# A two-layer hybrid decoder on one core: the mask and the gates' sums by adding transfers, rotary tables from the start, and later places for tasks behind long chains

## The chip, the cores and the metric

One core of one Trainium2 chip runs the whole program. The metric is the device time of one execution in microseconds, the median of the timed runs. The core's engines are TensorE (PE, matmuls, with its weight loads shown apart as PEld), VectorE (DVE), ScalarE (ACT), GpSimd (POOL) and SyncE (SP, which only issues loads of weights); 16 DMA engines move data. Each engine executes its own instructions in the order in which the program lists them.

## The reference

Two layers, each a mixer of three head groups, a cross-attention to 256 memory tokens and a SwiGLU feed-forward, all with sandwich RMSNorm, for 256 tokens of width 1024:

```python
def forgetting_attention(q, k, v, f_logit, b_f):
    ...
    log_f = jax.nn.log_sigmoid((f_logit + b_f).astype(jnp.float32))
    c = jnp.cumsum(log_f, axis=1).transpose(0, 2, 1)
    ...
        logits = jnp.einsum('bhqd,bhkd->bhqk', qb, k).astype(jnp.float32) * scale + cb[..., None] - c[:, :, None, :]
        q_pos = start + jnp.arange(Q_BLOCK)
        mask = key_pos[None, :] <= q_pos[:, None]
        p = jax.nn.softmax(jnp.where(mask, logits, -jnp.inf), axis=-1)
        return jnp.einsum('bhqk,bhkd->bhqd', p.astype(v.dtype), v)

def rotary(x, positions):
    half = x.shape[-1] // 2
    inv_freq = ROPE_THETA ** (-jnp.arange(half, dtype=jnp.float32) / half)
    ang = positions.astype(jnp.float32)[..., None] * inv_freq
    cos = jnp.cos(ang)[:, :, None, :]
    sin = jnp.sin(ang)[:, :, None, :]
    ...

def parallel_mixer(h, positions, w_in, conv_w, conv_b, w_rg, b_rg, w_ig, b_ig, lru_lambda, fox_b_f, w_out):
    proj = h @ w_in
    lx, ly, fq, fk, fv, ff, rq, rk, rv, rg = jnp.split(proj, np.cumsum(SPLIT_SIZES)[:-1].tolist(), axis=-1)
    lru_out = rg_lru(causal_depthwise_conv(lx, conv_w, conv_b), w_rg, b_rg, w_ig, b_ig, lru_lambda) * jax.nn.gelu(ly)
    fox_out = forgetting_attention(fq, fk, fv, ff, fox_b_f)
    ret_out = retention(rq, rk, rv, rg, positions)
    return jnp.concatenate([lru_out, fox_out.astype(h.dtype), ret_out], axis=-1) @ w_out
```

`retention` rotates its queries and keys by `rotary` before it multiplies them. The forgetting attention has 8 heads in blocks of 128 queries; a query sees no key after itself.

## The kernel before

Weights stream from DRAM in pieces of 128 partitions by 1024 floats (512 KB), issued on SP's queue into five raw buffers. Every piece is split into two parts that the matmuls can take with little loss: ACT makes `hi` (a cast of `raw`), DVE makes `lo` (`raw` minus `hi`). A product is then three matmuls: activation times hi, activation times lo, and the activation's own lower part times hi. There are eight pairs of hi and lo buffers, so pieces can be split some time ahead of their use.

The order of all instructions is found by a planner while the program is built (`Flow`). It keeps a clock for each engine, with estimated costs, and a heap of tasks, which are generators. A task that yields tensors is woken once the planner's clock of TensorE has passed the time at which it expects them to be written; a task that yields a number is woken that much later (`MARGIN` is 3.0 us). In between, TensorE gets the matmuls of the projections. What a woken task issues stands at that place of each engine's list. On the chip the engines keep to the list and wait for what their operands need: a bad estimate shows as a wait of TensorE. `pump` splits the next weight piece where the planner sees ACT and DVE free.

The tasks that the change touches:

- `rotary_tables` (L603): the positions' cast `s` on DVE, angles and their reduction `ang` on POOL (some 25 small instructions), Sin twice on ACT (`cs`), copies to `c` on DVE, four transposes of `c` on TensorE, and `turn` from them. With it `use_rqk` (L1008) makes `rab`, `rcd` and `rot` on DVE for the retention's queries and keys, and the scores `rsc` on TensorE.
- `gates` (L826): after the softplus of the forget gates (`soft`, a chain of small DVE instructions), three matmuls `cum` make the sums over tokens, which go to DRAM (`dr`, `cum<-cT`) and come back on POOL's queue, broadcast to all partitions, as four `far` tiles of 256 KB.
- `fox` (L874): the forgetting attention's logits `lg`. For each half of the queries and two heads' banks, a matmul of the identity with the mask (`lg<-maskb`, bfloat16, 0 or -1e30) starts the sum, the query-key matmuls add to it, and DVE scales it and adds `far` (`pexp<-lg,f,far`), takes the maximum and, behind ACT's Exp, divides.
- `lru` (L946): four matmuls `gate` in two banks, one bank after the other.
- `flip` in `ffn` (L1197): transposes of the gated hidden rows `fg`; `spread` (L776): norms as rows, `rsb<-diag`.
- `memory_norm` (L1256): mean squares of a memory half (`junk`, `ss`, `rstd`), the scaling `msrc<-msrc,rstd` on ACT, then transposes `tr<-cst,msrc`.

Of the kernel before, what the change touches and what calls it, by code (L numbers as in the profile page):

```python
# [18 lines left out]
P = 128  # L19
# [12 lines left out]
WORK_BUFS = 25  # L32
# [6 lines left out]
LATE = 6  # L39
TAIL = 2  # L40
# [16 lines left out]
def _constants():  # L57

    i = np.arange(P)
    gamma = 1.0 - np.exp2(-5.0 - np.arange(4, dtype=np.float64))  # L60
    diff = np.arange(SEQ)[None, None, :] - i[:, None, None]
    dec = np.where(diff >= 0, gamma[None, :, None] ** np.maximum(diff, 0), 0.0) * HD ** -0.5
    dec = np.concatenate([dec, dec[:, :, 0:P]], axis=2)
    inv = np.broadcast_to(10000.0 ** (-np.arange(32, dtype=np.float64) / 32), (P, 32))
    m = np.where(i[None, :] <= i[:, None], 0.0, NEG)
    z = np.zeros_like(m)
    mask = np.concatenate([m, m, m, m, z, m, z, m, np.eye(P)], axis=1)
    f = [np.eye(P), i[:, None] <= i[None, :], np.ones((P, P)), dec.reshape(P, -1), inv]
    return [np.asarray(x, np.float32) for x in f], mask.astype(ml_dtypes.bfloat16)
# [56 lines left out]
class Flow:  # L126
# [39 lines left out]
    def load(self, queue, out, ins=()):  # L166
# [6 lines left out]
        if queue == "POOL":  # L173

            self.swdge = max(t, self.clock["POOL"], self.swdge) + 2.0 * cost
            self.write(out, self.swdge + 1.3)
# [44 lines left out]
class Engine:  # L221
# [5 lines left out]
    def __getattr__(self, op):  # L227
        fn = getattr(self.eng, op)

        def call(*args, **kw):  # L230
# [5 lines left out]
            if "dma" in op:  # L236
                fn(*args, **kw)
                self.flow.load(self.name, outs[0], aps)
                return
# [47 lines left out]
def decoder(ctx: ExitStack, tc: tile.TileContext, a, out):  # L287
# [173 lines left out]
    def pump(force=False, later=None):  # L461
# [12 lines left out]
        if force or (idle and not flow.hold) or (here and lead < (LEAD if not flow.hold else HOLD_LEAD)):  # L474
# [8 lines left out]
            split(hi[:, 0:m], lo[:, 0:m], b.parts[i], later)  # L483
# [83 lines left out]
    maskb = const([P, 1024 + P], BF16, n="maskb")  # L567
    identb = maskb[:, 1024:1024 + P]
# [34 lines left out]
    def rotary_tables():  # L603
        posf = small([P, NT])
        V.tensor_copy(posf, posi)
# [35 lines left out]
        cs = work([P, 2, NT, 32], n="cs")  # L641
        S.activation(cs[:, 1], s, AF.Sin, bias=0.0, scale=1.0)
# [4 lines left out]
        yield c4  # L647
        tb = transposes([c4[:, c, t].rearrange("p h j -> p (h j)") for c in range(2) for t in range(NT)])
# [127 lines left out]
    def spread(xt, got):  # L776
# [7 lines left out]
        yield d  # L784
        b = bank("rsb")
# [6 lines left out]
    def mixer(l, xt, blk, skew, between=None):  # L792
# [10 lines left out]
        def use_fv_hi(t, q):  # L803
# [16 lines left out]
            if l == 0:  # L820
                PO.tensor_scalar(sp4, lfs[:, 0:4], -4.0, None, op0=ALU.mult)
                PO.tensor_scalar(sp2, lfs[:, 0:4], -2.0, None, op0=ALU.mult)
# [3 lines left out]
        def gates():  # L826


            yield list(lf)
            b = bank("cum")  # L830
# [8 lines left out]
            yield dr  # L839
            for e in range(2):  # L840
                for g in range(2):
                    far[e, g] = work([P, 2, SEQ], n="far")
                    PO.dma_start(out=far[e, g], in_=dr[4 * e + 2 * g:4 * e + 2 * g + 2, :].partition_broadcast(P))
# [30 lines left out]
        def fox(u):  # L874
# [7 lines left out]
            for e in range(2):  # L882
                matmul(bs[e], identb, maskb[:, 512 * t:512 * t + 512], True, False)
            for i, j in enumerate(js):
                for e in range(2):
                    r = slice(64 * e, 64 * e + 64)
                    matmul(bs[e][:, i * w:(i + 1) * w], qT[j // 2][r, j % 2, t * P:(t + 1) * P],
                           kT[j // 2][r, j % 2, 0:w], False, i == n - 1)
            ps = []
            for e in range(2):  # L890
# [4 lines left out]
                for g in sorted(set(j // 2 for j in js)):  # L895
                    i = 2 * g - js[0]
                    V.scalar_tensor_tensor(pv[:, i:i + 2], bv[:, i:i + 2], xt[t].by[HD ** -0.5], far[e, g][:, :, 0:w],
                                           op0=ALU.mult, op1=ALU.add)
# [47 lines left out]
        def lru():  # L946
# [18 lines left out]
            for gate, dst in ((0, tr), (1, ti)):  # L965
                b = bank("gate")
                for c in range(2):
                    matmul(b[:, c * SEQ:(c + 1) * SEQ], bd[:, l, gate, c, :], xc[:, c, :], True, True)
                for c in range(2):
                    o = 4 * gate + 2 * l + c  # L970
                    S.activation(dst[:, c, :], b[:, c * SEQ:(c + 1) * SEQ], AF.Tanh, bias=hb[:, o:o + 1], scale=0.5)
                yield 0.6
# [206 lines left out]
    def ffn(xt, blk, make_post):  # L1179
# [17 lines left out]
        def flip(t, gg):  # L1197
            tb = transposes([gg[:, j * P:(j + 1) * P] for j in range(4)])
# [3 lines left out]
            return  # L1202
            yield
# [52 lines left out]
    def memory_norm(m):  # L1256
# [9 lines left out]
        yield MARGIN  # L1266
# [37 lines left out]
    def between(k):  # L1304
# [7 lines left out]
        if t:  # L1312
            PO.dma_start(out=maskb, in_=a["mask"])
# [52 lines left out]
```

## Time and profile before

| | |
|---|---|
| median of three timed runs | 832.49 us (831.71 to 832.66) |
| the profiled run | 832.4 us, of which the span of its instructions is 830.6 us |
| mean granted clock of TensorE | 0.998 |
| DMA | 147.50 MB, mean 178 GB/s; 260 to 305 GB/s in the first three of 40 slices |
| DVE, lo<-raw,hi | 246 instructions, 293.9 us, 1.2 us each |
| ACT, hi<-raw | 246 instructions, 251.9 us, 1.0 us each |
| POOL's own DMA queue | 2080 packets, 7.91 MB |

A row of the timeline gives the start and the duration of an instruction (of several that follow each other without another between them: the whole, with their count), its engine and its line, and in brackets how long the engine had been idle before and what it waited for. Nearly all lines are those of helpers (L242 for all calls on DVE, ACT and POOL, L320 for matmuls, L341 for transposes), so instructions are told apart by the names of their tiles. Matmuls are pipelined: what one costs is the distance between starts, not its own duration. "DMA to landing" is the time from a transfer's issue to its completion.

### The profile page before, as it was taken

How to read it: one execution, taken by the hardware profiler on the slowest of the kernel's cores; microseconds unless marked ns; L12 is line 12 of the kernel's file. 1: busy time of each engine (PE TensorE's matmuls, PEld its weight loads, DVE VectorE, ACT ScalarE, POOL GpSimd, SP SyncE). 2: the span in 40 equal slices, each digit the busy share in tenths (PEclk: the TensorE clock that was granted, in tenths of full speed). 3: DMA queues.
4: the chain of work that ended last, by engine and by line, in shares of the span. 5: the costliest groups of instructions: out<-in, count | busy, mean ns of one | idle time of the engine just before them, and what ended most of it. 6: DMA issues, size and time to landing. Idle time of an engine off the chain costs nothing.

```text
span 830.6 us, 12999 instructions
## 1 busy us (share of the span) xinstructions
PE 818.8 (99%) x5023; PEld 714.9 (86%) x5023; DVE 588.9 (71%) x854; ACT 450.6 (54%) x728; POOL 80.2 (10%) x136
## 2 busy tenths in 40 slices
PE   9989999999999999999999999999999999999996
PEld 6989977998888888888889998789988788888885
DVE  6578996867577766758678888566767775857663
ACT  5569465746366544645474376555545563554541
POOL 2752100200020000000041100010002000000000
PEclk9999999999999999999999999999999999999999
DMA  8883545563357846557447563446444765647411
GB/s 296 305 260 121 171 158 155 188 216 114 121 185 240 251 138 220 186 157 232 137 128 237 168 204 127 151 129 228 145 129 133 232 222 181 207 147 244 139 49 51
DMA packets 101885, 147.50 MB, mean 178 GB/s; under 512 B 4976, under 2 KB 79104, under 8 KB 101696
## 3 DMA queue, kind: packets, MB, share of 16 engines
q1 hardware_dynamic: 99040, 138.17, 52.1%
q0 software_dynamic: 2080, 7.91, 2.8%
q8 instruction: 39, 0.64, 0.3%
q10 hardware_dynamic: 704, 0.59, 0.2%
q14 instruction: 22, 0.18, 0.1%
HBM read 145.59 MB, written 1.06 MB: 177 GB/s over the span
## 4 chain that ended last, share of the span: by engine, by line
PE 89%; DMA 3%; POOL 2%; issue 2%; DVE 2%; ACT 1%; DVEq 0%; POOLq 0%; ACTq 0%
PE acc L320 55%; PE dn L320 25%; PE tr L341 3%; DMA raw<-in_w_in 2%; PE co L320 1%; PE clg L320 1%; DMA raw<-in_w_down 1%; PE lg L320 1%; ACT hi L242 1%; POOL ang L242 1%; PE fo L320 1%; DVE lo L242 1%; PE ry L320 1%; POOL f L242 0%; PE gate L320 0%
## 5 line engine op out<-in xcount | busy, mean ns | idle before, releaser
L242 DVE TENSOR_TENSOR lo<-raw,hi 128x1024 fp32r<-128x1024 f32 (+2 forms) x246 | 293.9, 1215 | 88.1 <-ACT hi L242 86.7
L320 PE MATMUL acc<-xt,hi 128*128 128x256 f32 (+1 forms) x1344 | 340.1, 332 | 0.0
L242 ACT CAST hi<-raw 128x1024 fp32r<-128x1024 f32 (+2 forms) x246 | 251.9, 1043 | 92.5 <-PE acc L320 59.8
L320 PE MATMUL acc<-xt,lo 128*128 128x256 f32 x960 | 259.1, 282 | 0.0
L320 PEld LDWEIGHTS acc<-xt,hi 128*128 128x128 f32 x1344 | 223.3, 189 | 20.9 <-issue 0.4
L320 PEld LDWEIGHTS acc<-xt,lo 128*128 128x128 f32 x960 | 181.2, 189 | 6.3
L320 PE MATMUL acc<-hi,xt 128*128 128x512 f32 (+2 forms) x320 | 83.6, 351 | 0.0
L320 PEld LDWEIGHTS acc<-hi,xt 128*128 128x128 f32 x320 | 56.1, 188 | 8.5 <-ACT hi L242 0.6
L242 POOL TENSOR_TENSOR rp<-ssp,mh 128x1 f32<-128x1 f32 x12 | 6.8, 567 | 573.1 <-DVE ssp L242 573.0
L320 PE MATMUL acc<-lo,xt 128*128 128x512 f32 (+2 forms) x160 | 54.1, 349 | 0.0
L320 PE MATMUL dn<-hi,mth 128*128 128x512 f32 x128 | 51.6, 403 | 0.0
L242 DVE TENSOR_TENSOR fs<-acc,fs 128x256 f32<-128x256 f32 x72 | 30.1, 418 | 29.0 <-ACT fs L242 29.0
L320 PE MATMUL dn<-hi,mtl 128*128 128x512 f32 x128 | 50.5, 394 | 0.0
L320 PE MATMUL dn<-lo,mth 128*128 128x512 f32 x128 | 50.5, 394 | 0.0
L320 PE MATMUL acc<-mem,hi 128*128 128x256 f32 x256 | 47.3, 285 | 0.0
L242 ACT COPY fs<-acc 128x256 f32<-128x256 f32 x72 | 26.2, 364 | 37.7 <-PE acc L320 37.7
L320 PE MATMUL acc<-hi,mem 128*128 128x512 f32 x128 | 45.1, 405 | 0.0
L320 PE MATMUL dn<-hi,gh 128*128 128x512 f32 x112 | 44.3, 396 | 0.0
L320 PE MATMUL dn<-hi,gl 128*128 128x512 f32 x112 | 44.2, 394 | 0.0
L320 PE MATMUL dn<-lo,gh 128*128 128x512 f32 x112 | 44.2, 394 | 0.0
L320 PEld LDWEIGHTS acc<-mem,hi 128*128 128x128 f32 x256 | 39.5, 189 | 1.4 <-issue 1.0
L242 DVE TENSOR_TENSOR y<-dn,gpost 128x512 f32<-128x512 f32 x24 | 16.4, 685 | 28.3 <-ACT junk L242 28.3
(206 smaller groups left out, 1168.7 us busy)
## 6 DMA issues: line engine op xcount, KB each, us to landing
raw<-in_w_gate SPq DMA_DIRECT2D x44, 512.0 KB, 4.8
raw<-in_w_up SPq DMA_DIRECT2D x44, 512.0 KB, 4.6
raw<-in_w_down SPq DMA_DIRECT2D x44, 512.0 KB, 4.7
raw<-in_w_in SPq DMA_DIRECT2D x42, 512.0 KB, 5.4
raw<-in_w_ck SPq DMA_DIRECT2D x16, 512.0 KB, 3.7
raw<-in_w_cv SPq DMA_DIRECT2D x16, 512.0 KB, 4.9
raw<-in_w_out SPq DMA_DIRECT2D x16, 512.0 KB, 4.1
raw<-in_w_cq SPq DMA_DIRECT2D x16, 512.0 KB, 4.5
```

The costliest lines, as they stand in the source:

```text
L242: fn(*args, **kw)
L320: nc.tensor.matmul(out_ap, lhsT, rhs, start=start, stop=stop)
L341: nc.tensor.transpose(out_ap, src, ident[0:k, 0:k])
```

## The change

Six things, all within the functions above:

1. The mask matmuls are gone, and with them the mask's load (288 KB) and its tiles. The mask is now a float array in DRAM. In `gates`, six `far` tiles of 256 KB (one per bank of `lg`) are loaded with mask rows first (1.5 MB a layer), and six transfers of the sums are added to them in the transfer itself (`accum_op=ALU.add`) in place of the four plain ones. DVE's `pexp<-lg,f,far` is one instruction of 512 columns where it was two of 256.
2. `pump` makes the lower part of a piece in another way where the planner sees DVE late (between 60 and 130 us of its clock, with three pieces ready): ACT writes `lo = -hi`, and a transfer from DRAM adds the weights to it. In the built program this holds for four pieces, one of w_in and three of w_out.
3. The cast of positions is done by POOL, so the rotary angles don't wait for their place on DVE; both Sin stand together, and a MARGIN is put ahead of the transposes of `c`.
4. More waiting in the planner: MARGIN ahead of the `cum` matmuls and of the gate matmuls (less 1.0; both banks' matmuls now together), 0.7 us ahead of `flip` and of the matmul of `rsb`, MARGIN + 2 in place of MARGIN in `memory_norm`.
5. Two small instructions move from POOL to DVE (`sp4`, `sp2`, printed as `spl`), and there are 26 work buffers in place of 25.
6. The planner's estimate of the landing of a transfer on POOL's queue is longer (3.0 in place of 1.3).

```diff
@@ -29,7 +28,7 @@
 SPLIT_BUFS = 8
-WORK_BUFS = 25
+WORK_BUFS = 26
 PIECE = 1056
@@ -37,6 +36,7 @@
 LATE = 6
+DVE_LATE, ADD_LEAD, ADD_FROM, ADD_TO = 4.0, 3, 60.0, 130.0
 TAIL = 2
@@ -64,9 +64,9 @@
     z = np.zeros_like(m)
-    mask = np.concatenate([m, m, m, m, z, m, z, m, np.eye(P)], axis=1)
+    mask = np.concatenate([m, m, m, m, z, m, z, m], axis=1)
     f = [np.eye(P), i[:, None] <= i[None, :], np.ones((P, P)), dec.reshape(P, -1), inv]
-    return [np.asarray(x, np.float32) for x in f], mask.astype(ml_dtypes.bfloat16)
+    return [np.asarray(x, np.float32) for x in f], mask.astype(np.float32)
@@ -173,7 +173,7 @@
             self.swdge = max(t, self.clock["POOL"], self.swdge) + 2.0 * cost
-            self.write(out, self.swdge + 1.3)
+            self.write(out, self.swdge + 3.0)
             self.clock["DMA"] += cost
@@ -235,7 +235,7 @@
                 fn(*args, **kw)
-                self.flow.load(self.name, outs[0], aps)
+                self.flow.load(self.name, outs[0], aps + outs * ("accum_op" in kw))
                 return
@@ -480,7 +480,15 @@
                 flow.free[hi.tensor.name] = flow.free[lo.tensor.name] = freed["split"].pop(0)
-            split(hi[:, 0:m], lo[:, 0:m], b.parts[i], later)
+            hm, lm = hi[:, 0:m], lo[:, 0:m]
+            if ADD_FROM < flow.now < ADD_TO and c["DVE"] > c["PE"] + DVE_LATE and lead >= ADD_LEAD and c["POOL"] < c["PE"] + 4.0:
+
+                S.copy(hm, b.parts[i])
+                S.activation(lm, hm, AF.Copy, bias=0.0, scale=-1.0)
+                r, c0 = b.cuts[i], b.at[i]
+                PO.dma_start(out=lm.rearrange("p (c n) -> p c n", c=r), in_=b.src[:, c0:c0 + r, :], accum_op=ALU.add)
+            else:
+                split(hm, lm, b.parts[i], later)
             freed["raw"].append(flow.ready(lo) or flow.ready(hi) + 2.0)
@@ -564,8 +572,6 @@
     bd = cst[:, C_BD:C_END].rearrange("p (l g c j) -> p l g c j", l=DEPTH, g=2, c=2)
-    maskb = const([P, 1024 + P], BF16, n="maskb")
-    identb = maskb[:, 1024:1024 + P]
     minus_half = const([P, 4], n="mh")
@@ -602,7 +608,7 @@
         posf = small([P, NT])
-        V.tensor_copy(posf, posi)
+        PO.tensor_copy(posf, posi)
         ang, n1, n2, s, s2, m = (work([P, NT, 32], n="ang") for _ in range(6))
@@ -639,12 +645,14 @@
         cs = work([P, 2, NT, 32], n="cs")
+        yield s2
         S.activation(cs[:, 1], s, AF.Sin, bias=0.0, scale=1.0)
...
         yield c4
+        yield MARGIN
         tb = transposes([c4[:, c, t].rearrange("p h j -> p (h j)") for c in range(2) for t in range(NT)])
@@ -782,6 +790,7 @@
         yield d
+        yield 0.7
         b = bank("rsb")
@@ -818,8 +827,8 @@
             if l == 0:
-                PO.tensor_scalar(sp4, lfs[:, 0:4], -4.0, None, op0=ALU.mult)
-                PO.tensor_scalar(sp2, lfs[:, 0:4], -2.0, None, op0=ALU.mult)
+                V.tensor_scalar(sp4, lfs[:, 0:4], -4.0, None, op0=ALU.mult)
+                V.tensor_scalar(sp2, lfs[:, 0:4], -2.0, None, op0=ALU.mult)
                 V.tensor_scalar(hb, cols[:, L_BR:L_BR + 8], 0.5, None, op0=ALU.mult)
@@ -827,6 +836,11 @@
             yield list(lf)
+            yield MARGIN
+            for u, n in ((0, 4), (1, 2), (2, 2)):
+                for e in range(2):
+                    far[e, u] = work([P, n, 512 // n], n="far")
+                    PO.dma_start(out=far[e, u].rearrange("p j k -> p (j k)"), in_=a["mask"][:, 512 * (u > 0):512 * (u > 0) + 512])
             b = bank("cum")
@@ -836,11 +850,11 @@
             PO.dma_start(out=dr, in_=cT)
-            yield dr
-            for e in range(2):
-                for g in range(2):
-                    far[e, g] = work([P, 2, SEQ], n="far")
-                    PO.dma_start(out=far[e, g], in_=dr[4 * e + 2 * g:4 * e + 2 * g + 2, :].partition_broadcast(P))
+            yield [dr] + list(far.values())
+            for u, n, o in ((0, 4, 0), (1, 2, 0), (2, 2, 2)):
+                for e in range(2):
+                    r = 4 * e + o
+                    PO.dma_start(out=far[e, u], in_=dr[r:r + n, 0:512 // n].partition_broadcast(P), accum_op=ALU.add)
             got["far"] = 1
@@ -879,23 +893,18 @@
             bs = [bank("lg") for _ in range(2)]
-            for e in range(2):
-                matmul(bs[e], identb, maskb[:, 512 * t:512 * t + 512], True, False)
             for i, j in enumerate(js):
...
                     matmul(bs[e][:, i * w:(i + 1) * w], qT[j // 2][r, j % 2, t * P:(t + 1) * P],
-                           kT[j // 2][r, j % 2, 0:w], False, i == n - 1)
+                           kT[j // 2][r, j % 2, 0:w], True, True)
             ps = []
...
                 pv, bv = (x.rearrange("p (j k) -> p j k", j=n) for x in (p, bs[e]))
-                for g in sorted(set(j // 2 for j in js)):
-                    i = 2 * g - js[0]
-                    V.scalar_tensor_tensor(pv[:, i:i + 2], bv[:, i:i + 2], xt[t].by[HD ** -0.5], far[e, g][:, :, 0:w],
-                                           op0=ALU.mult, op1=ALU.add)
+                V.scalar_tensor_tensor(pv, bv, xt[t].by[HD ** -0.5], far[e, u], op0=ALU.mult, op1=ALU.add)
                 V.tensor_reduce(mx[t][:, o:o + n], pv, axis=AX, op=ALU.max, negate=True)
@@ -962,14 +971,15 @@
             yield xc
-            for gate, dst in ((0, tr), (1, ti)):
-                b = bank("gate")
+            yield MARGIN - 1.0
+            bg = [bank("gate") for _ in range(2)]
+            for gate, b in enumerate(bg):
                 for c in range(2):
                     matmul(b[:, c * SEQ:(c + 1) * SEQ], bd[:, l, gate, c, :], xc[:, c, :], True, True)
+            for gate, dst, b in ((0, tr, bg[0]), (1, ti, bg[1])):
                 for c in range(2):
...
                     S.activation(dst[:, c, :], b[:, c * SEQ:(c + 1) * SEQ], AF.Tanh, bias=hb[:, o:o + 1], scale=0.5)
-                yield 0.6
             yield [tr, ti]
@@ -1195,12 +1205,11 @@
         def flip(t, gg):
+            yield 0.7
             tb = transposes([gg[:, j * P:(j + 1) * P] for j in range(4)])
...
                 gt[t, k] = tuple(x[:, k * P:(k + 1) * P] for x in (h, l))
-            return
-            yield
@@ -1263,7 +1272,7 @@
         yield src
-        yield MARGIN
+        yield MARGIN + 2.0
         for c in range(2):
@@ -1310,7 +1319,6 @@
         if t:
-            PO.dma_start(out=maskb, in_=a["mask"])
             flow.spawn(late_loads())
```

The order of instructions as built. TensorE, first place: the projections of w_in around the matmuls `cum` (the forget gates' sums). Before, `cum` stands in the middle of the products of one piece:

```order
231 L320 MATMUL acc_651<-xt_103,lo_494 128x256
232 L320 MATMUL acc_651<-xt_103,hi_517 128x256 x2
233 L320 MATMUL acc_651<-xt_103,lo_518 128x256
234 L320 MATMUL cum_677<-cst_76,soft_83 8x128 x3
235 L320 MATMUL acc_651<-xt_103,hi_517 128x256 x2
```

Now, with `c` (the rotary tables) right behind:

```order
247 L320 MATMUL acc_662<-xt_102,lo_494 128x256
248 L320 MATMUL cum_736<-cst_76,soft_82 8x128 x3
249 L320 MATMUL acc_662<-xt_102,hi_525 128x256 x2
250 L320 MATMUL acc_662<-xt_102,lo_526 128x256
251 L341 MATMUL tr_747<-cst_76,c_609 128x128 x4
252 L320 MATMUL acc_662<-xt_102,hi_525 128x256 x2
```

Counted over the list, 159 projection matmuls of 256 columns stood ahead of `cum`, and 180 do now. The retention's scores `rsc` were behind 333 such matmuls, three groups of `msrc` transposes and four `gate` matmuls; they now are behind 240, two groups of `msrc` transposes and no `gate`.

DVE, the list around the rotary products `rab`, `rcd` and `rot`, which `rsc` needs (`xc` is the convolution, `lg<-lg,lyT` the gelu). Before:

```order
62 L242 TENSOR_TENSOR kT_847<-acc_742,rsb_528 128x512
63 L242 TENSOR_TENSOR lg_806<-lg_806,lyT_648 128x512
64 L242 TENSOR_TENSOR rab_868<-acc_421,turn_80 128x512
65 L242 TENSOR_TENSOR rcd_869<-acc_421,turn_80 128x512
66 L242 TENSOR_TENSOR rot_870<-rab_868 128x256
```

Now they follow the copy of the sums and the lower parts of three pieces:

```order
50 L242 TENSOR_TENSOR lxp_658<-acc_594,rsb_539 128x2x256
51 L242 TENSOR_TENSOR lo_687<-raw_500,hi_686 128x1024
52 L242 TENSOR_TENSOR lo_706<-raw_535,hi_705 128x1024
53 L242 TENSOR_TENSOR lo_721<-raw_563,hi_720 128x1024
54 L242 COPY cT_740<-cum_736 8x256
55 L242 TENSOR_TENSOR rab_754<-acc_435,turn_79 128x512
56 L242 TENSOR_TENSOR rcd_755<-acc_435,turn_79 128x512
57 L242 TENSOR_TENSOR rot_756<-rab_754 128x256
```

ACT makes `hi_705` and `hi_720` behind the scaling of the memory half, which waits for POOL:

```order
43 L242 ACTIVATE junk_679,ss_678<-msrc_104 128x1024
44 L242 CAST hi_686<-raw_500 128x1024
45 L242 ACTIVATE msrc_104<-msrc_104,rstd_677 128x1024
46 L242 CAST hi_705<-raw_535 128x1024
47 L242 CAST hi_720<-raw_563 128x1024
48 L242 COPY turn_79<-tr_747 128x512
```

TensorE, third place: the second `flip` of the first layer's feed-forward, with `rsb` behind it. Before:

```order
1254 L320 MATMUL acc_2985<-xt_103,hi_2857 128x512
1255 L320 MATMUL acc_2985<-xt_103,lo_2858 128x256
1256 L341 MATMUL tr_2988<-cst_76,fg_2907 128x128 x4
1257 L320 MATMUL rsb_2997<-diag_2960,cst_76 128x256
1258 L320 MATMUL acc_2985<-xt_103,lo_2858 128x256
```

Now it stands four matmuls later in the same product, two of 256 columns and two of 512, and the second layer shows the same:

```order
1239 L320 MATMUL acc_2989<-xt_102,hi_2861 128x512
1240 L320 MATMUL acc_2989<-xt_102,lo_2862 128x256 x2
1241 L320 MATMUL acc_2989<-xt_102,hi_2861 128x512
1242 L320 MATMUL acc_2989<-xt_102,lo_2862 128x256
1243 L320 MATMUL acc_2989<-xt_102,hi_2861 128x512
1244 L341 MATMUL tr_2996<-cst_76,fg_2911 128x128 x4
1245 L320 MATMUL rsb_3005<-diag_2964,cst_76 128x256
```

More of the change, by code (lines that the diff above doesn't have):

```diff
@@ L2 @@
 from contextlib import ExitStack
-import ml_dtypes
 import numpy as np
```

## The prediction

> **What bounds the kernel now.** I read the page first (span and engines), then the view of TensorE's waits, then its timeline around each wait.
>
> ```profile
> span 830.6 us, 12999 instructions
> PE 818.8 (99%) x5023; PEld 714.9 (86%) x5023; DVE 588.9 (71%) x854; ACT 450.6 (54%) x728; POOL 80.2 (10%) x136
> ...
> PE cum L320 <- DVE hb L242: 1.5, 1, 1.5
> PE tr L341 <- DVE fg L242: 1.4, 2, 0.8
> ...
> PE tr L341 <- DVE c L242: 1.0, 1, 1.0
> PE tr L341 <- ACT msrc L242: 0.4, 1, 0.4
> ```
>
> TensorE is busy for 818.8 of 830.6 us. So only two things can shorten the kernel: fewer matmuls, or fewer of these waits. The columns of the last four rows are total us, times and longest (a fifth, left out, is the program's start and stays); they make 1.5 + 1.4 + 1.0 + 0.4 = 4.3 us. The profiled run took 832.4 us, 1.8 us more than its span, and the median of the three timed runs is 832.49; I work against 832.4 and take the difference for nothing.
>
> A wait costs more than its idle time, because matmuls are pipelined:
>
> ```profile
> 45.73 0.40 PE L320 MATMUL acc<-xt,hi 128*128 128x256 f32 x2
> 45.97 0.28 PE L320 MATMUL acc<-xt,lo 128*128 128x256 f32 x1
> 47.70 0.49 PE L320 MATMUL cum<-cst,soft 128*8 128x128 f32 x3 [1.46 <-DVE hb L242]
> ```
>
> A 256-column matmul starts every 0.12 us (two from 45.73 to 45.97). `cum` starts 1.73 us after the one ahead of it: 1.61 us lost where the bracket says 1.46. With the same 0.15 on each of the five, the waits cost 1.6, 1.15 (c), 0.5 (msrc) and 0.75 + 0.9 (fg), 4.9 in all.
>
> **The change, part by part.**
>
> *The mask's matmuls go.*
>
> ```profile
> L320 PE MATMUL lg<-maskb 128*128 128x512 bf16 x12 | 3.6, 385 | 0.0
> ...
> 91.44 0.60 PE L320 MATMUL lg<-maskb 128*128 128x512 bf16 x2
> 91.97 0.83 PE L320 MATMUL lg<-kT,qT 64*128 64x128 f32 x10
> ```
>
> A pair takes TensorE from 91.44 to 91.97, 0.53 us; six pairs make **3.2 us**. TensorE is dense there, so all of it counts.
>
> *The margins.* `cum` stands 21 matmuls later (order, first place): 21 x 0.12 = 2.5 us, more than its 1.6. `c` and `msrc` are covered likewise: c is computed some 12 us earlier than now, and msrc's transposes stand MARGIN + 2 behind. The two `fg` transposes that wait stand four matmuls later, two of 0.12 and two of 0.23, 0.7 us: 0.05 and 0.2 remain, 1.4 goes. Gain 1.6 + 1.15 + 0.5 + 1.4 = **4.65 us**. What is late next is the following part.
>
> *The rotary scores become the next wait.* With tables ready early, the scores `rsc` move ahead on TensorE.
>
> ```profile
> 65.47 1.02 PE L320 MATMUL gate<-xc,cst 128*128 128x256 f32 x4
> 66.33 0.60 PE L341 MATMUL tr<-cst,msrc 128*128 128x128 f32 x4
> ...
> 74.58 1.59 PE L320 MATMUL rsc<-rot,rot 32*128 32x256 f32 x32
> ```
>
> `rsc` starts at 74.58. In the order it is moved past 93 matmuls of 0.12 (11.1 us), two such gate groups (0.86 each, 65.47 to 66.33) and one msrc transpose group (0.4): 13.2 us. Less the 3.3 us of cum, c and msrc, TensorE comes to it at 74.58 - 13.2 - 3.3 = 58.1. What it needs by then is a chain through DVE:
>
> ```profile
> 32.04 10.23 DMA raw<-in_w_in
> ...
> 42.29 1.05 ACT L242 CAST hi<-raw 128x1024 fp32r<-128x1024 f32 x1 [3.66 <-DMA raw<-in_w_in]
> ...
> 58.07 1.28 ACT L242 ACT_TABLE_LOAD   x1
> ...
> 43.37 1.23 DVE L242 TENSOR_TENSOR lo<-raw,hi 128x1024 fp32r<-128x1024 f32 x1 [3.75 <-ACT hi L242]
> ...
> 47.47 0.17 DVE L242 TENSOR_SCALAR hb<-cst 128x8 f32<-128x8 f32 x1
> ...
> 60.99 0.50 DVE L242 COPY c<-cs 128x256 f32<-128x256 f32 x2 [0.32 <-ACT cs L242]
> ...
> 51.91 2.42 POOL L242 TENSOR_SCALAR ss<-ss 128x1 f32<-128x1 f32 x1
> ...
> 55.01 1.15 ACT L242 ACTIVATE msrc<-msrc,rstd 128x1024 f32<-128x1024 f32 x1 [4.04 <-POOL rstd L242]
> ...
> 68.22 0.68 DVE L242 TENSOR_TENSOR rab<-acc,turn 128x512 f32<-128x512 f32 x1
> ...
> 71.62 0.41 DVE L242 TENSOR_TENSOR rot<-rcd 128x256 f32<-128x256 f32 x1
> ```
>
> The raw piece that is late (42.27) isn't moved by the change, so DVE ends its softplus with hb at 47.6 as before. Then two small ops (0.3), c (0.5), lo of two pieces (2.4), lxp (0.6), lo of three (3.6), cT (0.4) and the eight rotary ops (68.22 to 72.03, 3.8): 59.2. That is 1.1 after 58.1. But ACT makes the last two hi behind msrc, which waits for POOL's ss. On ACT the table load and both Sin (1.8 us) put the square sum at about 48.5. If ss takes 2.42 beside lo, as at 51.91, msrc starts 0.7 behind it (54.3 to 55.01) at 51.6 and ends at 52.7; two hi end at 54.7, lo at 56.0, then cT and rotary, 60.2: 2.1 after 58.1. I take the blocked ss, whose row is the nearest, and put **2.0**; ends 0.5 (a short ss, and 288 KB of mask no longer loaded ahead of the late piece, of whose 0.9 us at 332 GB/s, worked out below, half is gained) and 2.6 (msrc, two hi and the lo half a microsecond later). Queued behind it on TensorE is everything.
>
> *The rotary ops at the start* run on POOL from the landing of the positions on, beside DVE ops that TensorE then waits for directly. The landing, and what the two engines do to one another:
>
> ```profile
> L237 ACTq DMA_DIRECT2D posi<-in_positions x1: 456/456/456, 2.1 to 2.1; - x1
> ...
> DMA to landing us min/median/max: 5.3/5.3/5.3
> ...
> 22.20 3.29 POOL L242 TENSOR_SCALAR f<-rstd 128x1 f32<-128x1 f32 x5
> ...
> 28.29 1.35 POOL L242 TENSOR_SCALAR f<-rstd 128x1 f32<-128x1 f32 x5
> ...
> 55.06 0.40 POOL L242 TENSOR_SCALAR ang<-ang 128x64 f32<-128x64 f32 x1
> ...
> 22.12 2.36 DVE L242 TENSOR_TENSOR lo<-raw,hi 128x1024 fp32r<-128x1024 f32 x2 [0.77 <-ACT hi L242]
> ```
>
> They start at 2.1 + 5.3 = 7.4. POOL's five f take 3.29 us beside lo and 1.35 us with DVE idle; two lo beside them take 2.36, no more than the one at 43.37 with POOL idle (1.23). So POOL yields and DVE loses little. I put **0.3**, ends 0 and 0.7 (eight DVE ops by 0.08). POOL's own delay puts ss of the first tokens some 3 us later; it is needed by rvw and soft, several us ahead of their matmuls, so nothing.
>
> The Trainium skill, page "SBUF — State Buffer", section "SBUF: two separate sides", says that DVE with two SBUF inputs and a GpSimd op that reads SBUF hold one port pair as an exclusive lock, and the loser stands still for the whole instruction. The trace agrees as to POOL losing; no row shows DVE losing. By that rule the forecast would be some 3 us later (third rival).
>
> *The mask by adding transfers.*
>
> ```profile
> L237 POOL DMA_DIRECT2D far<-cum x8: 536/537/671, 64.6 to 452.8; - x8
> ...
> DMA to landing us min/median/max: 3.8/5.1/6.5
> ...
> L237 POOL DMA_DIRECT2D msrc<-in_mem x2: 527/528/530, 30.9 to 31.4; - x2
> ...
> DMA to landing us min/median/max: 7.6/8.8/10.1
> ...
> 97.03 0.87 DVE L242 SCALAR_TENSOR_TENSOR pexp<-lg,f,far 128x256 f32<-128x256 f32 x2
> ...
> 60.00:80.00 20.00, 19.01 (x173) 18.28 (x172) 16.21 (x33) 19.50 (x42) 5.17 (x10) 1.00 0.47 156
> ```
>
> The far tiles were issued at 64.6 and first read at 97.03; now six adding ones of the same size, read at about 92. The slack is over 25 us, and no row shows an adding transfer: at twice the slowest plain one, 20.2 us, they are still in time. The mask rows are 1.5 MB a layer, first at about 49 us. The last row (its last two numbers: share of the DMA engines, GB/s) gives 156 / 0.47 = 332 GB/s for full use, so 4.7 us; from 60 to 80 us the DMA engines are busy for 0.47 only and have room, and no weight piece is among TensorE's waits: nothing. Eight issues more a layer on POOL by 0.54 are 4.3 us of an engine that is 10% busy. Cost **0**.
>
> *Lower parts by adding transfers.* Four pieces; three are of w_out:
>
> ```profile
> 107.30 2.00 ACT L242 CAST hi<-raw 128x1024 fp32r<-128x1024 f32 x2
> ...
> 121.28 0.39 PE L320 MATMUL dn<-hi,mth 128*128 128x512 f32 x1
> ```
>
> From hi at 107.30 to the first use at 121.28 are 14 us. Less hi, the negated copy (1.05 each) and the issue (0.5), 11.4 us are left for the transfer. Plain ones of 512 KB took 7.6 to 10.1 on this queue: in time, **0**; at twice that, 20.2, 8.8 us late. I take 0, nearest to the plain rows, and keep the other end as a rival. DVE is spared 4 x 1.2 us in the stretch where it is full:
>
> ```profile
> 100.00:120.00 20.00, 20.00 (x124) 15.85 (x125) 19.37 (x32) 14.87 (x39) 0.00 (x0) 1.00 0.57 180
> ```
>
> (behind the length stand the busy times of TensorE, its loads and DVE). TensorE comes there 2.9 us earlier (3.3 + 1.6 of masks - 2.0), DVE has 3.7 us less of lo: about even, so nothing is put.
>
> **Sum:** 832.4 - 3.2 - 4.65 + 2.0 + 0.3 = **826.8 us**. Own range by the two bounds: 825.0 (0.5 and 0) to 827.8 (2.6 and 0.7).
>
> **The rivals.**
>
> *No new wait.* Tables early enough, ss unblocked, the late piece earlier: 832.4 - 7.85 = 824.5. Against it: the chain above is late by 1.1 even with a short ss. 15%.
>
> *DVE becomes the bound* in 80 to 120 us. For it: 19.4 of 20 us busy, and the waits that let DVE catch up (3.3 us) are gone. Against it: the lo it is spared. If the 2.9 us that TensorE gains there are all waited back at the transposes of pexp: 829.7. 13%.
>
> *POOL's rotary ops hold DVE up at the start.* About nine of them fit in ahead of 14.6 us (half of 7.2 us), 0.40 us each by the row of ang; were each to stop DVE once, where TensorE waits directly, 3.6 in place of 0.3: 830.1. Against it: DVE's 2.36 above. 7%. The page named above states this as its rule.
>
> *The waits only move.* The late piece lands later under the mask rows or the shifted POOL loads, and cum, c and msrc wait as they did (3.3): 830.1. Against it: cum is reached at 46.1 + 2.5 = 48.6, 1 us after hb. 7%.
>
> *Slower: adding transfers of w_out are slow.* It decides from 11.4 us a transfer; at 20.2 it adds 8.8 to the forecast: 835.6. For it: an add reads its destination too, and POOL issues beside a full DVE. Against it: all plain rows lie at 10.1 or below. 8%. The same page's section says that GpSimd writes the descriptors of such transfers and starves while DVE runs in a fast mode; far landing in 3.8 to 6.5 beside a DVE busy for 16.21 of 20 us speaks against a long starvation here.
>
> **How the numbers follow.** The forecast has the other 50%. Predicted is 826.8. A measurement of this kernel can tell about 0.2%, 1.7 us, so "same" is 830.8 to 834.1. Faster: 50 + 15 + 12 + 6 + 2, 85%; same, from the upper tails of the three rivals near 830, 8%; slower: 7% of the last one. The range of 823.5 to 831.0 holds all but the slow transfers and the ends of the cases near 830.
>
> **What would show it.** Right: no row of lg<-maskb; no wait of TensorE on hb, c or msrc, and at most 0.3 on fg; a new wait of 0.5 to 2.6 us at rsc for rot at about 58 us. far and lo landing below 11 us. The first 15 us the same within 0.7. Wrong: rows of pexp's transposes or of dn waiting for DVE or a DMA between 100 and 130 us; a wait at acc in the first 15 us; an adding transfer that lands in 12 us or more.

## The result, and the profile after

The changed kernel takes **826.11 us** (median of 4 runs, 825.88 to 826.53) against 832.29 for the kernel before on the same chip: a ratio of 0.9934, 95% interval 0.9922 to 0.9946. The forecast was 826.8 in a range of 823.5 to 831.0, faster. The profiled run's span is 824.6 us against 830.6. Of all the executions reported below, one of the kernel before (2082 us) and one of the mask alone (4594 us) lie far outside the others and are left out of the ratios.

The page's head, and behind it all waits of TensorE (total us, times, longest):

```profile
span 824.6 us, 12992 instructions
PE 815.6 (99%) x5011; PEld 714.8 (87%) x5011; DVE 584.6 (71%) x847; ACT 453.4 (55%) x732; POOL 94.4 (11%) x154
...
PE warm L320 <- DVE warm L242: 1.2, 1, 1.2
PE rsb L320 <- issue: 1.1, 1, 1.1
PE tr L341 <- DVE fg L242: 0.2, 1, 0.2
```

cum, c and msrc no longer wait, fg waits 0.2 where it waited 1.4, and no row has lg<-maskb. But the new wait isn't the one at `rsc` that was forecast: it stands at `rsb`, the norms turned into rows, 24 us earlier in the program. TensorE's timeline there, first of before, then of the change:

```profile
34.83 0.28 PE L320 MATMUL acc<-xt,lo 128*128 128x256 f32 x1
34.95 0.60 PE L320 MATMUL rsb<-diag,cst 128*128 128x256 f32 x2
```

```profile
34.55 0.28 PE L320 MATMUL acc<-xt,lo 128*128 128x256 f32 x1
35.95 0.67 PE L320 MATMUL rsb<-diag,cst 128*128 128x256 f32 x2 [1.13 <-issue]
```

rsb comes 1.40 us after the matmul ahead of it, where 0.12 was usual: 1.28 us lost. The bracket names no engine, so I followed the operand. rsb reads `diag`, which DVE writes from both halves' rstd. The chain in the changed kernel, on POOL, ACT and DVE in turn:

```profile
25.67 0.23 POOL L242 TENSOR_SCALAR ss<-ss 128x1 f32<-128x1 f32 x1
...
28.95 0.22 POOL L242 TENSOR_SCALAR ss<-ss 128x1 f32<-128x1 f32 x1
...
29.92 1.34 POOL L242 TENSOR_SCALAR f<-rstd 128x1 f32<-128x1 f32 x5
...
30.60 0.47 ACT L242 ACTIVATE rvw<-acc,f 128x256 f32<-128x256 f32 x1 [2.43 <-POOL f L242]
...
32.41 1.23 DVE L242 TENSOR_TENSOR lo<-raw,hi 128x1024 fp32r<-128x1024 f32 x1 [0.52 <-ACT hi L242]
...
35.38 0.47 DVE L242 TENSOR_SCALAR diag<-cst,rstd 128x128 f32<-128x128 f32 x2
```

The same two of before, ss of the second half and diag:

```profile
27.32 0.23 POOL L242 TENSOR_SCALAR ss<-ss 128x1 f32<-128x1 f32 x1
...
33.93 0.47 DVE L242 TENSOR_SCALAR diag<-cst,rstd 128x128 f32<-128x128 f32 x2
```

The first half's ss, which ran at 21.24 before, runs at 25.67, behind the rotary ops that now fill POOL from 7.60 on. The five f behind it then take 1.36 us, where they took 3.29 beside DVE's lo before, so the second half's ss is only 1.6 us later (28.95 against 27.32), and that is the delay that goes on. ACT's rvw of the second half waits 2.43 us for f, tg and the next hi stand behind it in ACT's list, lo<-raw,hi on DVE waits for that hi, and diag stands behind lo: it is written at 35.85 instead of 34.40. rsb starts at 35.95; TensorE could have started it at 34.67.

At rsc, TensorE comes 1.4 us later than forecast and finds rot ready:

```profile
59.30 0.28 PE L320 MATMUL acc<-xt,lo 128*128 128x256 f32 x1
59.51 1.59 PE L320 MATMUL rsc<-rot,rot 32*128 32x256 f32 x32
...
58.85 0.41 DVE L242 TENSOR_TENSOR rot<-rcd 128x256 f32<-128x256 f32 x1
```

rot is written at 59.26, rsc starts at 59.51. The two stretches in which DVE was full (length, then busy time of TensorE, its loads, DVE) now read:

```profile
80.00:100.00 20.00, 20.00 (x173) 19.24 (x172) 16.86 (x25) 14.07 (x21) 1.77 (x3) 1.00 0.64 212
100.00:120.00 20.00, 20.00 (x125) 16.55 (x125) 16.59 (x28) 19.35 (x50) 2.58 (x3) 1.00 0.82 214
```

DVE has 3 us of room in each, where it had 0.4 and 0.6. The adding transfers, by tile, with the use of the tightest one:

```profile
L237 POOL DMA_DIRECT2D far<-cum x12: 1389/2158/3019, 64.0 to 463.9; - x12
L242 DVE SCALAR_TENSOR_TENSOR pexp<-lg,f,far x12: 740/743/746, 94.3 to 516.0; 128x512 f32<-128x512 f32 x12
...
DMA to landing us min/median/max: 4.3/8.1/13.2
```

```profile
L237 POOL DMA_DIRECT2D lo<-in_w_out x3: 852/857/872, 106.8 to 115.0; - x3
L237 POOL DMA_DIRECT2D lo<-in_w_in x1: 1291/1291/1291, 72.3 to 72.3; - x1
...
DMA to landing us min/median/max: 8.6/9.2/11.0
...
108.83 0.86 POOL L237 DMA_DIRECT2D lo<-in_w_out  x1 [1.15 <-ACT lo L242]
...
120.41 0.39 PE L320 MATMUL dn<-lo,mth 128*128 128x512 f32 x1
```

The far tiles land at most 13.2 us after their issue (the last one of the second layer) and are read 30 us or more after it (94.3 against 64.0 for the first). The prediction had named an adding transfer that lands in 12 us or more as a sign of being wrong: it came, and cost nothing here. The second lower part of w_out has 11.6 us from issue (108.83) to use (120.41) and takes 11.0: in time by half a microsecond.

### The profile page after: what moved, and what is told of

Same layout as the page of the kernel before. It is cut to its first block, busy times and chain, and to the rows that moved or that the text cites. A ratio compares the mean times of both kernels' runs of the same rounds, so it can differ in the third digit from the quotient of the medians.

```text
span 824.6 us, 12992 instructions
## 1 busy us (share of the span) xinstructions
PE 815.6 (99%) x5011; PEld 714.8 (87%) x5011; DVE 584.6 (71%) x847; ACT 453.4 (55%) x732; POOL 94.4 (11%) x154
## 4 chain that ended last, share of the span: by engine, by line
PE 96%; issue 1%; DMA 1%; DVE 1%; ACT 0%; DVEq 0%; POOLq 0%; POOL 0%; ACTq 0%
PE acc L320 62%; PE dn L320 25%; PE tr L341 3%; PE clg L320 1%; PE co L320 1%; PE lg L320 1%; PE fo L320 1%; PE warm L320 1%; DMA raw<-in_w_down 1%; PE ry L320 1%; PE gate L320 0%; PE rsc L320 0%; ACT hi L242 0%; PE rsb L320 0%; DVE lo L242 0%
## 5 line engine op out<-in xcount | busy, mean ns | idle before, releaser
L242 DVE TENSOR_TENSOR lo<-raw,hi 128x1024 fp32r<-128x1024 f32 (+2 forms) x242 | 289.9, 1217 | 86.4 <-ACT hi L242 85.2
```

## The experiments

Times of the kernel before, run beside them, have medians of 831.83, 831.22 and 831.77 us for the three groups of experiments; between groups, and with the result above, the ratios are what compares. The edits are to the changed kernel unless something else is said.

### rsb later: did the wait at rsb hide one at rsc?

```diff
         yield d
-        yield 0.7
+        yield 0.7 if flow.now > 60.0 else 2.5
         b = bank("rsb")
```

> The changed kernel with rsb's matmuls 2.5 us (18 projection matmuls) later; cum, c, msrc and rsc keep their places in TensorE's list. Theory: the wait at rsb (1.13 us idle, 1.3 us between starts) comes from diag, which ends at 35.85 us, and has merely hidden the wait at rsc that the prediction put there: TensorE would come to rsc at 59.5 - 1.35 = 58.15, and rot is written at 59.26. So the wait at rsb goes, one of about 1.0 to 1.1 us on DVE's rot shows at rsc, and the time falls by 0.2 to 0.3 only, to about 825.9. Rival: the two have nothing to do with each other, no wait at rsc, 824.8.

Measured: 826.82 us (5 runs), ratio 0.9942 (0.9930 to 0.9954). TensorE's waits, and what made rot late, on POOL and ACT:

```profile
PE rsc L320 <- DVE rot L242: 2.1, 1, 2.1
...
49.35 1.19 POOL L242 TENSOR_SCALAR ss<-ss 128x1 f32<-128x1 f32 x1 [13.61 <-ACT junk L242]
50.62 1.40 POOL L242 TENSOR_TENSOR rstd<-ss,mh 128x1 f32<-128x1 f32 x1
...
52.05 1.15 ACT L242 ACTIVATE msrc<-msrc,rstd 128x1024 f32<-128x1024 f32 x1 [1.85 <-POOL rstd L242]
```

The wait at rsb is gone and the forecast's wait at rsc is there, at the forecast's size (2.0 put, 2.1 idle). The rival falls; the theory holds in kind, but at rsc it is 2.1 and not 1.0. msrc starts at 52.05 instead of 50.53 in the changed kernel: ss starts 0.7 us later there (the raw piece is 0.4 later, and the copy of rsb now stands in front on ACT), and ss and rstd take 2.7 us together beside DVE's lo, where in the changed kernel they take 1.8 (48.69 to 50.49). Removing the one wait gained nothing.

### rsb and rsc later

```diff
             yield list(rot)
+            yield 2.0
```

(with the edit above)

> As rsb_late, and 2.0 us in the planner ahead of the rsc matmuls, which then stand 18 projection matmuls (2.1 us) later. Theory: both waits are gone, 1.3 us less than the changed kernel, about 824.8. Rival (the wait moves on to the next consumer, gate or yc): no better than 825.9, with a wait of about 1 us between 60 and 80 us.

Measured: 829.68 us (10 runs, 827.03 to 830.92), ratio 0.9968 (0.9957 to 0.9979). Neither expected time. Of TensorE's waits, and of its timeline:

```profile
PE acc L320 <- DMA lo<-in_w_in: 1.1, 1, 1.1
...
83.20 0.28 PE L320 MATMUL acc<-hi,xt 128*128 128x256 f32 x1
84.58 0.39 PE L320 MATMUL acc<-lo,xt 128*128 128x256 f32 x1 [1.10 <-DMA lo<-in_w_in]
```

Both waits on DVE are gone, as expected, and the adding transfer of w_in is late: 11.9 us from issue to landing, where the changed kernel has 9.2. That is the mechanism of the prediction's slower rival, at another piece. The ten times fall into two groups: four up to 828.2 us with a mean granted clock of TensorE of 0.998 or 0.999, and six from 829.5 us on with 0.995 to 0.997.

### The same without adding transfers of weights

```diff
-DVE_LATE, ADD_LEAD, ADD_FROM, ADD_TO = 4.0, 3, 60.0, 130.0
+DVE_LATE, ADD_LEAD, ADD_FROM, ADD_TO = 4.0, 3, 60.0, 0.0
```

> rsb and rsc later as in rsb_rsc_late, and no adding transfers of weights. That run scattered from 827.0 to 830.9 us, and in its profile TensorE waited 1.1 us for lo<-in_w_in, which took 11.9 us to land. Theory: the adding transfer of w_in is what scatters and costs; without it the times lie within 1 us of each other, no wait on a transfer, 824.8. Rival: the scatter comes from the order around rsb and rsc or from the chip: it stays, median 827 or more.

Measured: 825.44 us (5 runs, 825.08 to 826.50), ratio 0.9931 (0.9919 to 0.9944). The scatter falls from 3.9 to 1.4 us, and the ratio by 0.0037, some 3 us; the expected 824.8 isn't quite reached. So the adding transfers made both, in this order; all of them are taken out, so which of them isn't shown. How much later they land in the runs at 830 isn't shown either, since the profiled run was one at 827.2. The lower clock in the six longer runs is likely part of their cost: 0.003 of 828 us would be 2.5 us (an estimate from the two groups of clocks).

### No adding transfers of weights, nothing else changed

(the same edit alone)

> The changed kernel with all lower parts made by DVE again (no adding transfer of weights; the mask's stay). The waits at rsb and fg stay. Theory: DVE has room, since PE waits for it nowhere between 80 and 130 us in the changed kernel, so the four adding transfers bought nothing: no change, 826.1 (within 0.5). Rival: DVE becomes the bound there without them: waits of TensorE on pexp, pT or lo between 90 and 130 us of up to 4 x 1.2 us, 827.5 or more.

Measured: 826.19 us (5 runs), ratio 0.9941 (0.9929 to 0.9953); no change. TensorE waits at rsb (1.2), no longer at fg, and, but for the start, nowhere for DVE; DVE is busy for 17.70 and 18.09 of 20 us in the two stretches, still below the 19.59 and 19.37 of before. The four adding transfers buy nothing in this kernel.

### The adding transfers issued later

```diff
+                if flow.now > 95.0:
+                    for _ in range(5):
+                        nc.gpsimd.tensor_scalar(scr, lm[:, 0:128].bitcast(F32), 1.0, 0.0, op0=ALU.mult, op1=ALU.add)
                 r, c0 = b.cuts[i], b.at[i]
                 PO.dma_start(out=lm.rearrange("p (c n) -> p c n", c=r), in_=b.src[:, c0:c0 + r, :], accum_op=ALU.add)
```

> The changed kernel with five small dummy instructions of POOL (128 columns of lo each, into a scratch tile) ahead of each of the three adding transfers of w_out; all other lists are the same. In the changed kernel they land 2.5, 0.54 and 5.7 us ahead of their first use. Theory: the margin is that small, so with a delay d of 1.5 to 2.5 us (0.3 to 0.5 each) the second piece makes TensorE wait d - 0.54, 1 to 2 us, and the time rises by as much, to 827 to 828. Rival: the landing doesn't follow the issue one to one (the queue or the DMA engines set it), and less than 0.5 us shows.

Measured: 827.99 us (8 runs, 827.38 to 831.08), ratio 0.9966 (0.9955 to 0.9978). On POOL and TensorE:

```profile
113.97 0.89 POOL L237 DMA_DIRECT2D lo<-in_w_out  x1 [0.30 <-POOL scr L490]
...
121.88 0.50 PE L320 MATMUL dn<-lo,mth 128*128 128x512 f32 x1 [1.19 <-DMA lo<-in_w_out]
```

The dummies took 2.4 to 3.3 us for each transfer, so the second one is issued 5.1 us later than in the changed kernel (113.97 against 108.83), but lands only 2.0 us later (121.83 against 119.87): issued 4.2 us behind the first it needs 7.9 us, issued 2.0 us behind it needed 11.0. That the two disturb each other is likely, but not shown apart from the rest. The wait is 1.2 us, and the time rises by 1.9 us between the medians (2.7 by the ratios). Two of the eight runs, at 830.0 and 831.1 us, again have a lower mean clock (0.997; the others 0.998 or 0.999). The margin is as thin as the trace said, but a landing doesn't follow its issue one to one.

### The rotary tail behind the norms

```diff
         yield n2
+        while not nrm[1].scaled:
+            yield 0.3
         for n, part in ((n2, d1), (n1, t4), (n2, d2), (n1, t5), (n2, d3), (n1, t6)):
```

> The changed kernel with the second half of the rotary ops on POOL held back until both token halves have their norms, so that ss, rstd and f stand ahead of it. Theory: the rotary ops ahead of ss on POOL are what made f, with it rvw, tg, the next hi and lo, and so diag late. Then f of the first half starts near 22 (26.6 in the changed kernel), the second rvw near 29.9 (31.47) and diag ends near 34.3 (35.85). The planner moves rsb earlier here (behind 144 projection matmuls instead of 162, at about 32.5 us), so the wait at rsb stays in sum, about 1.8 us, though diag is earlier. Rival: diag is late for the weight pieces or DVE's own queue: diag still ends at 35.5 or later.

Measured: 825.63 us (4 runs), ratio 0.9933 (0.9919 to 0.9947), span 823.4. On POOL, DVE and TensorE:

```profile
21.73 0.22 POOL L242 TENSOR_SCALAR ss<-ss 128x1 f32<-128x1 f32 x1 [2.98 <-ACT junk L242]
...
27.02 1.34 POOL L242 TENSOR_SCALAR f<-rstd 128x1 f32<-128x1 f32 x5
...
31.33 0.48 DVE L242 TENSOR_SCALAR diag<-cst,rstd 128x128 f32<-128x128 f32 x2
...
32.54 0.59 PE L320 MATMUL rsb<-diag,cst 128*128 128x256 f32 x2
```

ss runs at 21.73, nearly as before the change, and diag is written at 31.81, 4.0 us earlier than in the changed kernel and more than expected, so rsb doesn't wait although it stands 18 matmuls earlier. Of the 4.0 us, 2.9 come through POOL (the second ss runs at 26.07 instead of 28.95); the rest is one lo less ahead of diag on DVE in this order. The 2.9 alone would have done, as the changed kernel's wait is 1.28. But for the start, its list of waits has none for DVE or ACT left. This shows the cause of the wait at rsb: the rotary ops ahead of ss on POOL. The time doesn't show a gain by itself: the ratio is that of the changed kernel, and the four runs lie between 824.91 and 827.35 us.

### The tail behind the norms, without adding transfers

(the edit above, and `ADD_TO` at 0.0)

> rot_tail_late (825.6, no wait of TensorE left but the start's) without the adding transfers of weights. Theory: they buy nothing here either: 825.3, within 0.5 of rot_tail_late, with less scatter between its runs (824.9 to 827.4 there). Rival: DVE is missed: waits between 80 and 130 us and 826.5 or more.

Measured: 825.70 us (5 runs, 825.34 to 826.49), ratio 0.9935 (0.9923 to 0.9946). No loss, less scatter; 0.4 us of wait at rsc.

### flip without its 0.7 us

```diff
         def flip(t, gg):
-            yield 0.7
+            yield 0.0
```

> The changed kernel without the 0.7 us ahead of flip. Theory: the fg transposes stand as before and wait 0.75 and 0.9 us again; the changed kernel has 0.24 left of that, so 1.2 to 1.4 us slower, 827.4. Rival: the gain came from what moved elsewhere, no change.

Measured: 827.21 us (5 runs), ratio 0.9945 (0.9933 to 0.9957). The medians lie 1.1 us apart, but the ratios only 0.9 us, with overlapping intervals, and fg waits 0.36 us in one layer and not at all in the other, while rsb waits 1.4 us where the changed kernel has 1.1. So the expected waits didn't come back: that the 0.7 us are worth 1.2 isn't shown, and most of the 1.4 came from elsewhere in the order.

### The mask by adding transfers alone

The kernel before with the parts of the diff that concern far, maskb and pexp, and with 26 work buffers.

> The kernel before with the mask by adding transfers alone (no margins, rotary as before, no lower parts by adding). Theory: the twelve mask matmuls were worth 3.2 us and nothing takes it back: 3.2 below before, 1.15 more if the c transposes, which the planner puts 99 projection matmuls later here, no longer wait; the waits at cum (1.5) and fg (1.4) stay. Ratio 0.9948 to 0.9962. Rival: adding transfers are late or disturb the weights, and less than 2 us is left.

Measured: 830.19 us (median of 11 runs), ratio 0.9979 (0.9970 to 0.9988), span 828.0: 1.7 us by the ratio, 2.6 by the spans, and not 3.2. TensorE's waits and DVE's busy time:

```profile
PE tr L340 <- ACT msrc L241: 1.1, 1, 1.1
PE cum L319 <- DVE hb L241: 0.8, 1, 0.8
...
PE fo L319 <- ACT pT L241: 0.5, 1, 0.5
PE dn L319 <- DVE mtl L241: 0.4, 1, 0.4
...
80.00:100.00 20.00, 20.00 (x192) 18.94 (x192) 19.69 (x37) 11.00 (x25) 1.41 (x1) 1.00 0.53 156
100.00:120.00 20.00, 20.00 (x125) 16.18 (x124) 19.62 (x34) 11.99 (x26) 1.18 (x1) 1.00 0.47 158
```

The mask's matmuls are gone and c's wait with them, but DVE stays full from 80 to 120 us, and TensorE, coming sooner, waits behind it: 0.9 us at mtl and pT that the kernel before didn't have. So the prediction's rival that DVE becomes the bound is real for this part alone; this run's own rival has the size right by the ratio, but no adding transfer is among TensorE's waits. The account doesn't close: with two waits at fg of 0.8 together, the waits but the start's add up to 3.6 us where they were 4.3, so 3.2 + 0.7 should have gone. The span fell by 2.6, and the other 1.3 aren't assigned.

### Rotary started by DVE again

```diff
         posf = small([P, NT])
-        PO.tensor_copy(posf, posi)
+        V.tensor_copy(posf, posi)
```

> The changed kernel with the positions' cast on DVE again, so that POOL's rotary ops start at about 14.8 instead of 7.9 us and fewer of them stand ahead of ss. Theory: the early start is worth nothing by itself; it only put POOL in the way of ss. Then diag ends 1.5 us earlier or more, no wait at rsb, none at rsc (which the planner puts 63 projection matmuls later), and DVE's first ops take as long as before the change (xt 0.65 each where the changed kernel has 0.73, four lo at 12.5 us 3.7 in all where it has 3.89): about 824.9. Rival: the tables are needed early: a wait at c or rsc of 1 us or more, 826 or above.

Measured: 836.94 us (6 runs, 836.58 to 839.83), ratio 1.0073 (1.0062 to 1.0085): slower than before the change. My theory falls. TensorE's waits:

```profile
PE acc L320 <- DMA lo<-in_w_ck: 3.2, 1, 3.2
PE rsc L320 <- DVE kT L242: 1.9, 2, 1.7
PE rsc L320 <- DVE rot L242: 1.4, 1, 1.4
...
PE gate L320 <- DVE xc L242: 1.2, 1, 1.2
```

The first half of the theory holds: diag is written at 34.55, 1.3 us earlier, and rsb doesn't wait. But with late tables rab, rcd and rot stand between xc and kT on DVE at 64 to 75 us, where DVE is busy for 9.8 of 10 us, and gate and rsc wait there; an adding transfer, one of six in this order, is 3.2 us late besides. These waits, with one of 0.5 that isn't shown, are 8.2 us, and the changed kernel has 1.3 in their place, but the span of the profiled run, the longest of the six, is 13.4 us longer. More than half of the rest is in TensorE's granted clock (the third number from the end of a row):

```profile
75.00:80.00 5.00, 4.97 (x36) 4.52 (x37) 2.42 (x5) 4.97 (x8) 1.20 (x2) 0.50 1.13 221
...
110.00:115.00 5.00, 3.26 (x17) 3.26 (x18) 4.03 (x8) 1.28 (x5) 0.00 (x0) 0.73 1.08 303
```

Behind the waits at rsc, and again behind the late transfer, the granted clock is low for some microseconds, where the changed kernel has 1.00. By the two rows, 0.50 and 0.27 of 5 us, that is 3.9 us, an estimate. So the early start is worth much in this order: it brings the rotary products ahead of that stretch of DVE. How much of the 11 us between the medians is its own, and how much the late transfer's, isn't separated.

### The changed kernel again, and the best version

The best version is tail_no_add, with 1.0 us in the planner ahead of rsc.

> The changed kernel as it is, on the same chip as the next three, for comparison: 826.1 within 0.5, with the wait at rsb of 1.1 to 1.4 us.

> rot_tail_late without adding transfers of weights, and rsc 9 projection matmuls later, past the 0.4 us wait that tail_no_add had there. Theory: no wait of TensorE is left but the start's, span about 823.3, time 825.1, 1 us below the changed kernel on the same chip, with runs within 1 us of each other. Rival: as fast as tail_no_add (825.7) because something else waits in its place.

Measured on one chip: the changed kernel 826.11 us (5 runs, 825.35 to 826.77), ratio 0.9933 (0.9921 to 0.9946), with 1.0 us at rsb, just under the expected 1.1; the best version **824.92 us** (4 runs, 824.66 to 825.20), ratio 0.9921 (0.9909 to 0.9934), with no wait of TensorE in the list but the start's. Every run of it is below every run of the changed kernel, though the intervals of the ratios overlap. It leaves the change's second part out (lower parts by adding) and is 1.2 us faster.

## Why the prediction was right, point by point

- **Mask, 3.2 us:** the twelve matmuls left the trace, and TensorE is dense where they stood. That fits the whole change; alone it showed 1.7 by the ratio. The prediction took the parts as independent, and they aren't: alone, TensorE meets a full DVE. What makes the room in the whole change wasn't isolated; it isn't the four lower parts, as DVE keeps 2 us of room in each stretch without them.
- **Margins, 4.65 us:** cum, c and msrc don't wait any more, as said; that each owes this to its own margin wasn't tried. fg keeps 0.24 us, as said, but flip_back ascribes only part of it to flip's 0.7 us.
- **rsc, 2.0 us, is the step that failed as put.** The changed kernel has no wait there. Two things were wrong. The blocked ss that was chosen (2.42 us) didn't come: ss took 0.32 and rot was written at 59.26, so that by these numbers TensorE, coming at 58.1, would have waited 1.1 and not 2.0. And TensorE came later, because 1.28 us were lost at rsb, which was costed at nothing: "POOL's own delay puts ss of the first tokens some 3 us later; it is needed by rvw and soft, several us ahead of their matmuls, so nothing." ss of the first half was 4.4 us later and that of the second 1.6, and the consumer that mattered was a third, diag: in the kernel before rsb started 0.55 us after diag was written, so a delay of 1.45 was too much. That the sum came out nearly right, a wait of 1.28 in place of one of 2.0, is luck. rsb_late shows that the one wait hid the other: with rsb out of the way, rsc waits 2.1 us, though with a longer ss than the changed kernel's.
- **Start, 0.3 us:** the first of TensorE's waits on DVE there moved from 11.14 to 11.21. DVE's ops beside POOL's rotary ops, first before, then after:

```profile
11.00 1.29 DVE L242 TENSOR_TENSOR xt<-xg,xt 128x512 fp32r<-128x512 f32 x2
```

```profile
11.08 1.45 DVE L242 TENSOR_TENSOR xt<-xg,xt 128x512 fp32r<-128x512 f32 x2
```

  Two xt take 0.16 us more, far from the 0.40 us of a whole POOL op each. The rival by the rule of the Trainium skill, page "SBUF — State Buffer", section "SBUF: two separate sides", that the loser stands still for the whole instruction, shows on POOL (f five times in 3.29 or in 1.34 us) and not on DVE.
- **The late raw piece** "isn't moved by the change": hi of it started at 42.91 instead of 42.29, probably for the delay of lo on DVE ahead of it, which frees the raw buffers. Small; rot was written at 59.26, where the sum with a short ss had 59.2.
- **Adding transfers, nothing:** right in cost, but the landings weren't below 11 us as said: far took up to 13.2 and had 30. For w_out the budget was 11.4 us and is 11.6; the three transfers took 8.6 to 11.0, just inside. The rival on the other side, given 8%, was nearer than its chance: two other orders of the same kernel ran into it, with 1.1 and 3.2 us, and so did the one with delayed issues, with 1.2.
- **DVE in 80 to 120 us, about even:** it was idle for 1.0 us there and is for 6.5, and without the adding transfers still for 4.2. So most of the room isn't from the lower parts. The rotary products ran at 68 to 72 us and now end at 59, so that what stood behind them can run earlier; that this makes the room is likely, but no run isolates it.

By the terms that showed, -3.2 - 4.65 + 1.28 + 0.07 makes -6.5; the spans differ by 6.0. The remaining 0.5 us is spread over small gaps and isn't assigned.

## What to carry to other kernels

When work is moved earlier onto an idle engine, list everything that stands behind it in that engine's queue, and follow each to the next engine that takes its result in order, to the last consumer; "several us of slack" has to be a row for every one of them. A wait that is removed uncovers the next one only if TensorE arrives sooner than its operand, so two waits in series can be worth less than their sum (here one hid the other). A transfer that is just in time in the profiled run is a source of scatter: price its margin, not its mean. And look at the granted clock before a loss is put down to waits alone: in start_dve some 4 us of it were matmuls that ran slower behind the waits.

## What the runs showed of the hardware

Six broadcast transfers that add occupy POOL's queue for 6.30 us, from the first start to the last end:

```profile
64.01 6.30 POOL L237 DMA_DIRECT2D far<-cum  x6
```

Six plain loads of 256 KB, the mask rows at 50.45, took 3.31 us there, and the four plain broadcasts of before 2.27. The records of the adding ones last 1.4 to 3.0 us each, but they overlap: the next starts 0.5 to 0.9 us later. In the first layer they landed 1.25 to 1.6 us apart.

From 60 to 125 us of the changed kernel the queues show (packets, MB, share of the DMA engines' time):

```profile
q1 hardware_dynamic: 6194, 10.21, 49.0%
q0 software_dynamic: 2758, 4.23, 36.0%
```

q0 is POOL's queue, nearly all of it adding transfers there (3.7 of 4.2 MB); q1 has the plain weight pieces. At about the same packet size a megabyte on q0 takes 8.5% of that time and one on q1 4.8%; in the same stretch of the kernel before, where nothing adds, q0 took 7.3% for 1.58 MB, 4.6% a megabyte. In the window from 60 to 80 us the mean share of the DMA engines reads 1.12. It reads 1.04 from 50 to 60 us of start_dve too, where no adding transfer is under way: that column can exceed 1 and isn't a utilisation.

In start_dve the granted clock of TensorE read 0.50 from 75 to 80 us, behind 10 us in which TensorE had been busy for 5.0, and 256-column matmuls then started 0.21 us apart, where 0.12 is usual. It read 0.73 from 110 to 115 us, behind a wait of 3.2 us. Behind single waits of 1.1 to 2.1 us (rsb in the changed kernel, rsc in rsb_late, the late transfers of rsb_rsc_late and slow_add) it read 1.00.
